# The start of the second attention lane in a two-layer decoder kernel, tied to the first lane by an event, with a shorter stated latency for one norm

## The chip, the cores and the metric

The kernel runs on one core of a Trainium2 chip. The metric is the time of one execution on the device in microseconds (us). The engines of the core run side by side, each through its own queue of instructions, and wait for one another by semaphores: PE (TensorE, matrix products and transposes), DVE (VectorE), ACT (ScalarE), POOL (GpSimd) and SP (SyncE, which here only starts transfers).

## The reference

A stack of two layers over 256 positions of width 1024. Each layer adds to the residual stream, every time behind an RMS norm: half a gated feed-forward, a mixer, a cross attention over 256 memory tokens, and half a second feed-forward. The mixer is the part that the change touches:

```
z = h @ w_in                     # one projection: HGRN2 q|f|i|g, FoX q|k|v, forget logits
o_h = hgrn2_chunk_scan(...)      # 4 heads, then a norm per head and a gate
s = q k^T / 8 + (c_t - c_s)      # FoX: 8 heads x 64, c = running sum of log forget gates
o_f = softmax(causal(s)) v
x += concat(o_h, o_f) @ w_out
# cross attention, on the same x:
x += softmax(rms_norm(x) wq (rms_norm(mem) wk)^T / 16) (rms_norm(mem) wv) wo
```

## The kernel before

Everything is computed in float32 on PE with the operands split in two parts, a high and a low one, so that each product is three matmuls (`mm3`, L455 to L457; L455 uses both high parts, L456 and L457 a low one). The weights are loaded in pieces of 1 MB by SP (tiles `raw`, 3 buffers, L145). ACT casts a piece to the high part (`whi`, L158, or L162 when a gain is multiplied in) and DVE takes the difference as the low part (`wlo`, L159 or L163); 7 buffers of each. Activations are split alike by `put_split` (L380): the high part by ACT (L381), the low part by DVE (L382). So `xfh`/`xfl`, `oTh`/`oTl`, `mfh`/`mfl` (the memory's features) and the two halves of `kc` (the cross attention's keys) come about.

The causal FoX attention works on pairs of heads. Two tasks, the lanes, run `fox_lane`: lane 0 takes pair 0 and then pair 2, lane 1 pairs 1 and 3. For a pair a lane stacks its operands (`fox_stack`), makes the scores of two heads (`fs`, L966, one small PSUM tile for each head), takes the row maxima on DVE (`fmx`, L973, which is also the last reader of `fs`) and negates them (`fnm`, L977), takes exponentials on ACT (L928), reciprocals (`frc`, L930) and the normalisation of the probabilities `pp` on DVE (L932), transposes them on PE (`fpt`, L984), copies the transposes by ACT (`ppT`, L987), multiplies by the values (`fpv`, L997 to L999) and splits the result into `oTh`/`oTl`. The HGRN2 heads end beside it (L868 on DVE, transposes `hot`, L874).

While the lanes work, the mixer's main task fills PE with products for the cross attention, which need only the memory: keys (`acc` of 128x256, then `kc`) and values (`acc` of 128x512). Then come the product with `w_out`, the residual, and the norm for the cross attention, one `norm_task` for each half of the positions: square, gain and inverse root, then after a stated latency the transposes (`to_feat`, `pt`, L375) and the split into `xfh`/`xfl`.

The order of the instructions on every engine is that of recording. `drive` lets tasks take turns by a virtual clock that only counts PE's time: a task that yields a number moves the clock on, one that yields a tuple sleeps for that many microseconds while others record (a stated latency), and one that yields an `Event` sleeps until it is fired, and `fire(lat)` wakes it `lat` after the clock at that moment. So a constant such as `LAT_LANE` or `LAT_X` costs no time itself; it sets what is recorded ahead of what. Within this order a scheduler puts some norm and split instructions earlier on their engines (`tc.high_priority`). The small PSUM tiles (`fs`, `fpt`, `fpv`, `hot`, `pt` and others) share 4 buffers in turn, so each waits until the fourth before it has been read for the last time.

Before the change lane 1 sleeps after its first `fox_stack` for `LAT_FK + LAT_LANE` = 6.5 + 2.8, lane 0 for 6.5, each from when it was recorded itself.

## Time and profile before

| | us |
|---|---|
| median of 3 runs | 1210.65 |
| lowest and highest of them | 1210.35, 1213.19 |
| the profiled execution | 1210.42 |
| its span, first to last instruction | 1208.6 |
| PE busy | 1194.0 |
| DVE busy | 769.2 |
| ACT busy | 651.4 |
| POOL busy | 37.7 |

The mean granted clock of TensorE was 0.999 of full speed. A row of the timeline gives start, duration, engine, source line, operation, the tile written and those read, the shape and how many instructions were merged; a bracket tells how long the engine sat idle ahead of it and who released it. Matmuls are pipelined: one of 128x256 lasts 0.28 us but the next starts 0.11 us after it, so stalls on PE are read from the starts. Layer 0's mixer attention lies at about 295 to 330 us, its norm at 343 to 367; layer 1's at about 885 to 926 and 938 to 962.

### The profile page before, as it was taken

The numbers are of one execution on the slowest core, as the hardware profiler recorded it, in microseconds if no ns is written. First come the engines' busy times: TensorE is split into PE (matmuls) and PEld (weight loads), VectorE is DVE, ScalarE is ACT, GpSimd is POOL, SyncE is SP. The second block draws the span as 40 slices with busy tenths as digits, with TensorE's granted clock in tenths as the row PEclk, the third lists the DMA queues.
The fourth block names the chain that finished last, engine by engine and source line by source line (L and its number), as shares of the span: only waits on it lengthen the run. The fifth ranks groups of instructions, "written<-read, shape, count | busy, mean of one in ns | idle before, by whom it ended". The sixth has DMA issues, their size and how long they took to land.

```text
span 1208.6 us, 21485 instructions
## 1 busy us (share of the span) xinstructions
PE 1194.0 (99%) x8989; PEld 1094.6 (91%) x8989; DVE 769.2 (64%) x1194; ACT 651.4 (54%) x1022; POOL 37.7 (3%) x50
## 2 busy tenths in 40 slices
PE   9999999999999999999999999999999999999997
PEld 7999888989889889998889998889988898999986
DVE  6866647488866675565474565476787766555643
ACT  7556535578854464454354454266687555444532
POOL 0000000011000000000000000000110000000000
PEclk9999999999999999999999999999999999999999
DMA  8655655544444374565474666464445533555750
GB/s 300 226 192 177 240 175 185 184 142 140 166 165 175 105 261 145 204 214 205 139 259 143 209 209 210 139 222 163 145 154 169 190 130 137 192 194 175 244 174 36
DMA packets 100001, 218.66 MB, mean 181 GB/s; under 512 B 4128, under 2 KB 16704, under 8 KB 99904
## 3 DMA queue, kind: packets, MB, share of 16 engines
q1 hardware_dynamic: 99744, 217.03, 53.0%
q8 instruction: 70, 1.15, 0.4%
q10 hardware_dynamic: 160, 0.27, 0.1%
q14 instruction: 27, 0.22, 0.1%
HBM read 216.23 MB, written 1.05 MB: 180 GB/s over the span
## 4 chain that ended last, share of the span: by engine, by line
PE 86%; DVE 6%; ACT 4%; issue 2%; DMA 2%; POOL 1%; POOLq 0%; SPq 0%; ACTq 0%; DVEq 0%
PE acc L455 26%; PE acc L456 26%; PE acc L457 26%; DVE wlo L159 2%; ACT whi L162 1%; DVE wlo L163 1%; PE acc L520 1%; DMA mem<-in_mem_dram 1%; PE pt L375 1%; DMA raw<-in_w_in_dram 1%; POOL rs L356 1%; ACT whi L158 1%; DVE xfl L382 0%; PE al L797 0%; ACT pp L928 0%
## 5 line engine op out<-in xcount | busy, mean ns | idle before, releaser
L159 DVE TENSOR_TENSOR wlo<-raw,whi 128x1024 fp32r<-128x1024 f32 (+1 forms) x332 | 389.8, 1196 | 256.6 <-ACT whi L158 247.8
L158 ACT CAST whi<-raw 128x1024 fp32r<-128x1024 f32 (+1 forms) x332 | 331.8, 1030 | 258.8 <-PE acc L457 148.6
L457 PE MATMUL acc<-xfh,wlo 128*128 128x256 f32 x1536 | 424.4, 276 | 1.4 <-DVE wlo L159 1.3
L455 PE MATMUL acc<-xfh,whi 128*128 128x256 f32 x1536 | 425.6, 277 | 0.0
L456 PE MATMUL acc<-xfl,whi 128*128 128x256 f32 x1536 | 424.3, 276 | 0.7 <-DVE xfl L382 0.7
L457 PEld LDWEIGHTS acc<-xfh,wlo 128*128 128x128 f32 x1536 | 288.3, 188 | 2.0 <-DVE wlo L159 2.0
L456 PEld LDWEIGHTS acc<-xfl,whi 128*128 128x128 f32 x1536 | 288.4, 188 | 1.4 <-DVE xfl L382 1.1
L455 PEld LDWEIGHTS acc<-xfh,whi 128*128 128x128 f32 x1536 | 288.4, 188 | 0.9 <-ACT whi L158 0.2
L455 PE MATMUL acc<-whi,hth 128*128 128x512 f32 (+1 forms) x352 | 136.9, 389 | 0.0
L457 PE MATMUL acc<-whi,htl 128*128 128x512 f32 (+1 forms) x352 | 136.4, 387 | 0.0
L456 PE MATMUL acc<-wlo,hth 128*128 128x512 f32 (+1 forms) x352 | 136.3, 387 | 0.0
L455 PE MATMUL acc<-whi,xfh 128*128 128x512 f32 (+1 forms) x240 | 87.5, 365 | 0.0
L457 PE MATMUL acc<-whi,xfl 128*128 128x512 f32 (+1 forms) x240 | 86.8, 362 | 0.0
L456 PE MATMUL acc<-wlo,xfh 128*128 128x512 f32 (+1 forms) x240 | 86.6, 361 | 0.0
L457 PEld LDWEIGHTS acc<-whi,htl 128*128 128x128 f32 x352 | 66.1, 188 | 13.6
L456 PEld LDWEIGHTS acc<-wlo,hth 128*128 128x128 f32 x352 | 66.1, 188 | 13.2
L455 PEld LDWEIGHTS acc<-whi,hth 128*128 128x128 f32 x352 | 66.1, 188 | 13.2
L163 DVE SCALAR_TENSOR_TENSOR wlo<-raw,g,whi 128x512 fp32r<-128x512 f32 (+1 forms) x96 | 62.0, 701 | 20.9 <-ACT whi L162 20.9
L162 ACT ACTIVATE whi<-raw,g 128x512 fp32r<-128x512 f32 (+1 forms) x96 | 58.3, 677 | 19.3 <-PE acc L456 15.2
L457 PEld LDWEIGHTS acc<-whi,xfl 128*128 128x128 f32 x240 | 45.1, 188 | 7.3
L381 ACT CAST hth<-sil 128x512 fp32r<-128x512 f32 x36 | 22.3, 620 | 54.0 <-DVE sil L760 53.9
L456 PEld LDWEIGHTS acc<-wlo,xfh 128*128 128x128 f32 x240 | 45.2, 188 | 6.8
(274 smaller groups left out, 1520.3 us busy)
## 6 DMA issues: line engine op xcount, KB each, us to landing
raw<-in_ffn_w_down_dram SPq DMA_DIRECT2D x44, 1024.0 KB, 5.0
raw<-in_ffn_w_up_dram SPq DMA_DIRECT2D x40, 1024.0 KB, 5.4
raw<-in_ffn_w_gate_dram SPq DMA_DIRECT2D x38, 1024.0 KB, 5.2
raw<-in_w_in_dram SPq DMA_DIRECT2D x24, 1024.0 KB, 5.3
raw<-in_cross_wk_dram SPq DMA_DIRECT2D x8, 1024.0 KB, 5.2
raw<-in_cross_wv_dram SPq DMA_DIRECT2D x8, 1024.0 KB, 5.3
raw<-in_w_out_dram SPq DMA_DIRECT2D x8, 1024.0 KB, 4.9
raw<-in_cross_wq_dram SPq DMA_DIRECT2D x8, 1024.0 KB, 5.1
```

The lines of the kernel that those rows point to most:

```text
L158: nc.scalar.copy(out=hi, in_=sl)
L159: nc.vector.tensor_tensor(out=lo, in0=sl, in1=hi.bitcast(F32), op=ALU.subtract)
L162: nc.scalar.mul(hi, sl, g)
L163: nc.vector.scalar_tensor_tensor(out=lo, in0=sl, scalar=g, in1=hi.bitcast(F32), op0=ALU.mult, op1=ALU.subtract)
L356: nc.gpsimd.tensor_tensor(out=rs, in0=ms, in1=neghalf[:, 0:1], op=ALU.pow)
L375: nc.tensor.transpose(pt[:, j * P:(j + 1) * P], hn[:, kt * P:(kt + 1) * P], ident)
L381: nc.scalar.copy(out=hi, in_=src)
L455: nc.tensor.matmul(ps, lhsT=lh, rhs=rh, start=start, stop=False)
L456: nc.tensor.matmul(ps, lhsT=lh, rhs=rl, start=False, stop=False)
L457: nc.tensor.matmul(ps, lhsT=ll, rhs=rh, start=False, stop=stop)
L520: nc.tensor.matmul(psa_[t], lhsT=x, rhs=w, start=kt == 0 and which == 0, stop=kt == KT - 1 and which == 1)
```

## The change

Two things change. The norm behind the mixer is created with a stated latency of 5.3 in place of 6.5. And lane 1, before its first scores, sleeps 6.5 like lane 0 and then waits for an event that lane 0 fires when its own first scores and softmax are recorded, with a latency of 2.0; the stated 2.8 is gone.

```
-LAT_NORM, LAT_X = 5.5, 6.5
+LAT_NORM, LAT_X = 5.5, 5.3
...
-LAT_FK, LAT_LANE = 6.5, 2.8
+LAT_FK, LAT_LANE = 6.5, 2.0
...
-    def fox_lane(lane, fq, fk, fv, L_, R_, oT, cmask, oh, ready, done):
+    def fox_lane(lane, fq, fk, fv, L_, R_, oT, cmask, oh, ready, done, ahead):
         yield ready
         for pr in (lane, lane + 2):
             qs, ks = fox_stack(pr, fq, fk, L_, R_, oh)
-            yield (LAT_FK + LAT_LANE * (pr == 1),)
+            yield (LAT_FK,)
+            if pr == 1:
+                yield ahead
             prs = []
             for sub in range(2):
                 ps = smp("fs")
...
                 softmax(pr_, nmx, 1.0, [(t, pr_[:, o:o + n], pr_[:, o:o + n]) for t, o, n in SEGS])
+            if pr == 0:
+                ahead.fire(LAT_LANE)
             yield (LAT_FS,)
...
+        ahead = Event()
         for lane in range(2):
-            spawn(fox_lane(lane, fq, fk, fv, L_, R_, oT, cmask, oh, ev_g, ev_p))
+            spawn(fox_lane(lane, fq, fk, fv, L_, R_, oT, cmask, oh, ev_g, ev_p, ahead))
```

No instruction is added or removed on any engine; their order moves on PE, DVE, ACT and SP. Lines of the changed kernel below the lanes' first change are 2 to 5 higher: L966 becomes L968, L973 L975, L977 L979, L984 L988.

The first place is DVE in layer 0, second pair: the rows between the maxima of lane 1 (heads' probabilities `pp_526` and `pp_532`) and their normalisations L932. Before:

```order
L163 SCALAR_TENSOR_TENSOR wlo_543_3855<-raw_491_3580,gmem_202_1659,whi_542_3854 128x512
L977 TENSOR_SCALAR fnm_534_3818<-fmx_533_3815 128x2
L163 SCALAR_TENSOR_TENSOR wlo_543_3855<-raw_491_3580,gmem_202_1659,whi_542_3854 128x512
L159 TENSOR_TENSOR wlo_554_3911<-raw_496_3594,whi_553_3910 128x1024
L930 RECIPROCAL frc_530_3805<-fsm_529_3802 128x2
L930 RECIPROCAL frc_536_3823<-fsm_535_3820 128x2
L932 TENSOR_SCALAR pp_526_3796<-pp_526_3796,frc_530_3805 128x128
L932 TENSOR_SCALAR pp_526_3796<-pp_526_3796,frc_530_3805 128x256
L932 TENSOR_SCALAR pp_532_3814<-pp_532_3814,frc_536_3823 128x128
L932 TENSOR_SCALAR pp_532_3814<-pp_532_3814,frc_536_3823 128x256
L382 TENSOR_TENSOR kc_433_3270<-acc_512_3721,kc_432_3269 128x512
L159 TENSOR_TENSOR wlo_556_3915<-raw_496_3594,whi_555_3914 128x1024
```

After:

```order
L163 SCALAR_TENSOR_TENSOR wlo_543_3855<-raw_491_3580,gmem_202_1659,whi_542_3854 128x512
L979 TENSOR_SCALAR fnm_534_3821<-fmx_533_3818 128x2
L159 TENSOR_TENSOR wlo_554_3911<-raw_496_3594,whi_553_3910 128x1024
L930 RECIPROCAL frc_530_3808<-fsm_529_3805 128x2
L159 TENSOR_TENSOR wlo_556_3915<-raw_496_3594,whi_555_3914 128x1024
L932 TENSOR_SCALAR pp_526_3799<-pp_526_3799,frc_530_3808 128x128
L932 TENSOR_SCALAR pp_526_3799<-pp_526_3799,frc_530_3808 128x256
L930 RECIPROCAL frc_536_3826<-fsm_535_3823 128x2
L382 TENSOR_TENSOR kc_433_3270<-acc_512_3721,kc_432_3269 128x512
L932 TENSOR_SCALAR pp_532_3817<-pp_532_3817,frc_536_3826 128x128
L932 TENSOR_SCALAR pp_532_3817<-pp_532_3817,frc_536_3826 128x256
```

A second weight split (`wlo_556`) and the split of `kc_433` now stand ahead of the last two L932, and the reciprocal of the second head stands behind the first head's L932.

The second place is layer 1, first pair, on PE: the scores of lane 0 (`fs_1365`, `fs_1371`) and of lane 1. Before:

```order
L966 MATMUL fs_1365_9605<-fks_1340_9449,fqs_1339_9448 128x128 x2
L966 MATMUL fs_1365_9605<-fks_1340_9449,fqs_1339_9448 128x256 x2
L966 MATMUL fs_1371_9623<-fks_1340_9449,fqs_1339_9448 128x128 x2
L966 MATMUL fs_1371_9623<-fks_1340_9449,fqs_1339_9448 128x256 x2
L966 MATMUL fs_1377_9641<-fks_1342_9465,fqs_1341_9464 128x128 x2
L966 MATMUL fs_1377_9641<-fks_1342_9465,fqs_1341_9464 128x256 x2
L966 MATMUL fs_1383_9659<-fks_1342_9465,fqs_1341_9464 128x128 x2
L966 MATMUL fs_1383_9659<-fks_1342_9465,fqs_1341_9464 128x256 x2
L455 MATMUL acc_1389_9679<-mfh_1265_8775,whi_1328_9392 128x256
L456 MATMUL acc_1389_9679<-mfl_1266_8776,whi_1328_9392 128x256
L457 MATMUL acc_1389_9679<-mfh_1265_8775,wlo_1329_9393 128x256
```

After, from 18 matmuls behind lane 0's scores on (lane 1's are `fs_1378` and `fs_1384` now):

```order
L455 MATMUL acc_1377_9643<-mfh_1267_8777,whi_1346_9488 128x256
L456 MATMUL acc_1377_9643<-mfl_1268_8778,whi_1346_9488 128x256
L457 MATMUL acc_1377_9643<-mfh_1267_8777,wlo_1347_9489 128x256
L968 MATMUL fs_1378_9665<-fks_1342_9465,fqs_1341_9464 128x128 x2
L968 MATMUL fs_1378_9665<-fks_1342_9465,fqs_1341_9464 128x256 x2
L968 MATMUL fs_1384_9683<-fks_1342_9465,fqs_1341_9464 128x128 x2
L968 MATMUL fs_1384_9683<-fks_1342_9465,fqs_1341_9464 128x256 x2
L455 MATMUL acc_1377_9643<-mfh_1267_8777,whi_1346_9488 128x256
L456 MATMUL acc_1377_9643<-mfl_1268_8778,whi_1346_9488 128x256
L457 MATMUL acc_1377_9643<-mfh_1267_8777,wlo_1347_9489 128x256
```

Lane 1's scores stood right behind lane 0's; now 21 matmuls of the keys' product lie between. In the same place on DVE, from lane 1's first normalisation (`pp_1378` before, `pp_1379` after) to the first split of the next weight; `wlo_1396` is the low part of the last weight block of the keys' product that PE works on there. Before:

```order
L932 TENSOR_SCALAR pp_1378_9646<-pp_1378_9646,frc_1382_9655 128x128
L932 TENSOR_SCALAR pp_1378_9646<-pp_1378_9646,frc_1382_9655 128x256
L163 SCALAR_TENSOR_TENSOR wlo_1396_9753<-raw_1343_9480,gmem_202_1659,whi_1395_9752 128x512 x2
L930 RECIPROCAL frc_1388_9673<-fsm_1387_9670 128x2
L932 TENSOR_SCALAR pp_1384_9664<-pp_1384_9664,frc_1388_9673 128x128
L932 TENSOR_SCALAR pp_1384_9664<-pp_1384_9664,frc_1388_9673 128x256
L382 TENSOR_TENSOR oTl_1357_9565<-hot_1390_9713,oTh_1356_9564 128x4x128
L382 TENSOR_TENSOR oTl_1357_9565<-hot_1391_9720,oTh_1356_9564 128x4x128
L382 TENSOR_TENSOR kc_1336_9445<-acc_1389_9679,kc_1335_9444 128x512
L163 SCALAR_TENSOR_TENSOR wlo_1399_9761<-raw_1348_9494,gmem_202_1659,whi_1398_9760 128x512 x2
```

After:

```order
L163 SCALAR_TENSOR_TENSOR wlo_1396_9753<-raw_1343_9480,gmem_202_1659,whi_1395_9752 128x512
L930 RECIPROCAL frc_1383_9679<-fsm_1382_9676 128x2
L932 TENSOR_SCALAR pp_1379_9670<-pp_1379_9670,frc_1383_9679 128x128
L932 TENSOR_SCALAR pp_1379_9670<-pp_1379_9670,frc_1383_9679 128x256
L930 RECIPROCAL frc_1389_9697<-fsm_1388_9694 128x2
L932 TENSOR_SCALAR pp_1385_9688<-pp_1385_9688,frc_1389_9697 128x128
L932 TENSOR_SCALAR pp_1385_9688<-pp_1385_9688,frc_1389_9697 128x256
L382 TENSOR_TENSOR oTl_1357_9565<-hot_1390_9713,oTh_1356_9564 128x4x128
L382 TENSOR_TENSOR oTl_1357_9565<-hot_1391_9720,oTh_1356_9564 128x4x128
L382 TENSOR_TENSOR kc_1336_9445<-acc_1377_9643,kc_1335_9444 128x512
L163 SCALAR_TENSOR_TENSOR wlo_1396_9753<-raw_1343_9480,gmem_202_1659,whi_1395_9752 128x512
```

The second half of `wlo_1396` stood ahead of the last two normalisations and now stands behind them, both `oTl` and the split of `kc`.

The third place is PE at the norm behind the mixer, layer 0, second half of the positions (the transposes `pt_614` and `pt_615`; layer 1 and the first half alike). Before:

```order
L457 MATMUL acc_599_4149<-whi_601_4152,mfl_349_2551 128x512
L455 MATMUL acc_598_4148<-whi_603_4158,mfh_348_2550 128x512
L456 MATMUL acc_598_4148<-wlo_604_4159,mfh_348_2550 128x512
L457 MATMUL acc_598_4148<-whi_603_4158,mfl_349_2551 128x512
L455 MATMUL acc_599_4149<-whi_603_4158,mfh_348_2550 128x512
L456 MATMUL acc_599_4149<-wlo_604_4159,mfh_348_2550 128x512
L457 MATMUL acc_599_4149<-whi_603_4158,mfl_349_2551 128x512
L375 MATMUL pt_614_4228<-ident_101,hn_605_4170 128x128 x4
L375 MATMUL pt_615_4235<-ident_101,hn_605_4170 128x128 x4
L455 MATMUL acc_598_4148<-whi_603_4158,mfh_348_2550 128x512
L456 MATMUL acc_598_4148<-wlo_604_4159,mfh_348_2550 128x512
```

After:

```order
L457 MATMUL acc_599_4149<-whi_601_4152,mfl_349_2551 128x512
L375 MATMUL pt_614_4222<-ident_101,hn_605_4170 128x128 x4
L375 MATMUL pt_615_4229<-ident_101,hn_605_4170 128x128 x4
L455 MATMUL acc_598_4148<-whi_603_4158,mfh_348_2550 128x512
L456 MATMUL acc_598_4148<-wlo_604_4159,mfh_348_2550 128x512
L457 MATMUL acc_598_4148<-whi_603_4158,mfl_349_2551 128x512
L455 MATMUL acc_599_4149<-whi_603_4158,mfh_348_2550 128x512
L456 MATMUL acc_599_4149<-wlo_604_4159,mfh_348_2550 128x512
L457 MATMUL acc_599_4149<-whi_603_4158,mfl_349_2551 128x512
L455 MATMUL acc_598_4148<-whi_603_4158,mfh_348_2550 128x512
L456 MATMUL acc_598_4148<-wlo_604_4159,mfh_348_2550 128x512
```

The transposes stand six matmuls of 128x512 earlier. On ACT and DVE the splits into `xfh` and `xfl` now stand ahead of the casts and splits of the third piece of `cross_wq` (`whi_626`, `wlo_627`), and on SP the load of the next gain vector (`wn`) ahead of the load of that piece.

Further moves of the same kind: in layer 0 the first scores, transposes and value products of lane 1 and its second scores stand three matmuls of 128x256 later; in its first pair the split `kc_431` and one negation stand on DVE ahead of lane 1's second maximum. In layer 1 lane 1's first transposes stand 24 matmuls behind lane 0's (before 3), its value products 18 behind (before adjacent), its second scores behind six matmuls of 128x512 more, its second transposes 12 of these behind lane 0's and the value products 6 behind (both adjacent before).

## Rows read from the trace of the kernel before

**Rows 1.** The page of the profile: its first line, PE's busy time with its share of the span and its count of instructions, and the shares of engines in the chain of work that ended last.

```profile
span 1208.6 us, 21485 instructions
...
PE 1194.0 (99%) x8989; PEld 1094.6 (91%) x8989; DVE 769.2 (64%) x1194; ACT 651.4 (54%) x1022; POOL 37.7 (3%) x50
...
PE 86%; DVE 6%; ACT 4%; issue 2%; DMA 2%; POOL 1%; POOLq 0%; SPq 0%; ACTq 0%; DVEq 0%
```

**Rows 2.** The list of waits of PE: for what it waited, in all (us), how often, and the longest.

```profile
PE fs L966 <- DVE AX L868: 1.0, 1, 1.0
PE acc L456 <- DVE xfl L382: 0.7, 2, 0.4
PE fpt L984 <- DVE oTl L382: 0.7, 1, 0.7
...
PE fpv L997 <- ACT ppT L987: 0.3, 1, 0.3
```

**Rows 3.** The timeline of PE at the norm behind the mixer, layer 0.

```profile
364.70 1.04 PE L375 MATMUL pt<-ident,hn 128*128 128x128 f32 x8
...
366.96 0.40 PE L455 MATMUL acc<-xfh,whi 128*128 128x256 f32 x2
367.72 0.39 PE L456 MATMUL acc<-xfl,whi 128*128 128x256 f32 x1 [0.36 <-DVE xfl L382]
```

**Rows 4.** The timeline of DVE at the same place.

```profile
361.30 5.76 DVE L159 TENSOR_TENSOR wlo<-raw,whi 128x1024 fp32r<-128x1024 f32 x5
366.98 1.28 DVE L382 TENSOR_TENSOR xfl<-pt,xfh 128x512 fp32r<-128x512 f32 x2
```

**Rows 5.** The timeline of SP at the same place: the issue of the load of the next gain vector.

```profile
358.87 0.34 SPq L350 DMA_DIRECT2D wn<-in_ffn_norm_dram  x1
```

**Rows 6.** The timeline of PE in layer 0: the lanes' first pairs, and below the second.

```profile
298.88 0.84 PE L984 MATMUL fpt<-ident,pp 128*128 128x128 f32 x6
299.47 0.36 PE L455 MATMUL acc<-mfh,whi 128*128 128x256 f32 x1
...
303.50 0.43 PE L997 MATMUL fpv<-ppT,fv 128*64 128x128 f32 x2
...
304.57 0.38 PE L455 MATMUL acc<-mfh,whi 128*128 128x256 f32 x1
...
306.29 0.28 PE L457 MATMUL acc<-mfh,wlo 128*128 128x256 f32 x1
306.87 0.43 PE L997 MATMUL fpv<-ppT,fv 128*64 128x128 f32 x2 [0.30 <-ACT ppT L987]
...
323.98 0.82 PE L984 MATMUL fpt<-ident,pp 128*128 128x128 f32 x6
324.55 0.47 PE L455 MATMUL acc<-whi,mfh 128*128 128x512 f32 x1
```

**Rows 7.** The timeline of DVE in layer 0: the first pairs, and below the second.

```profile
298.69 0.42 DVE L973 CUSTOM_DVE_ANT_0 pp<-fs,cmask 128x256 f32<-128x256 f32 x1
...
299.32 0.67 DVE L382 TENSOR_TENSOR kc<-acc,kc 128x512 fp32r<-128x512 f32 x1
...
321.94 1.22 DVE L159 TENSOR_TENSOR wlo<-raw,whi 128x1024 fp32r<-128x1024 f32 x1
...
323.26 1.01 DVE L932 TENSOR_SCALAR pp<-pp,frc 128x128 f32<-128x128 f32 x4
324.19 0.68 DVE L382 TENSOR_TENSOR kc<-acc,kc 128x512 fp32r<-128x512 f32 x1
324.79 4.62 DVE L159 TENSOR_TENSOR wlo<-raw,whi 128x1024 fp32r<-128x1024 f32 x4
```

**Rows 8.** The timeline of PE in layer 1: the first pairs, and the transposes of the second.

```profile
886.18 1.17 PE L966 MATMUL fs<-fks,fqs 128*128 128x128 f32 x8
888.40 1.28 PE L966 MATMUL fs<-fks,fqs 128*128 128x128 f32 x8 [1.05 <-DVE AX L868]
...
897.18 0.28 PE L457 MATMUL acc<-mfh,wlo 128*128 128x256 f32 x1
898.17 1.14 PE L984 MATMUL fpt<-ident,pp 128*128 128x128 f32 x6 [0.72 <-DVE oTl L382]
899.08 0.36 PE L455 MATMUL acc<-mfh,whi 128*128 128x256 f32 x1
...
902.00 0.43 PE L997 MATMUL fpv<-ppT,fv 128*64 128x128 f32 x2
...
903.73 0.39 PE L455 MATMUL acc<-mfh,whi 128*128 128x256 f32 x1
...
918.66 1.47 PE L984 MATMUL fpt<-ident,pp 128*128 128x128 f32 x12
```

**Rows 9.** The timeline of DVE in layer 1: the first pairs, and below the second.

```profile
895.45 1.41 DVE L163 SCALAR_TENSOR_TENSOR wlo<-raw,gmem,whi 128x512 fp32r<-128x512 f32 x2
...
898.63 0.68 DVE L382 TENSOR_TENSOR kc<-acc,kc 128x512 fp32r<-128x512 f32 x1
899.24 2.73 DVE L163 SCALAR_TENSOR_TENSOR wlo<-raw,gmem,whi 128x512 fp32r<-128x512 f32 x4
...
918.79 0.54 DVE L932 TENSOR_SCALAR pp<-pp,frc 128x128 f32<-128x128 f32 x2
919.25 3.49 DVE L159 TENSOR_TENSOR wlo<-raw,whi 128x1024 fp32r<-128x1024 f32 x3
```

## The prediction

> **What bounds the kernel now.** I read the page first: TensorE (PE) is busy 99% of the 1208.6 us span and holds 86% of the chain of waits [rows 1]. No matmul is added or removed, so the time can change only by the few microseconds in which PE waits, and by new waits of the same kind. The list of PE's waits comes second [rows 2]: it holds some 8 us, and four of its entries lie where the change moves something: the scores (fs) behind L868, the transposed probabilities (fpt) behind L382, the values product (fpv) behind ppT, and the first matmuls of the cross attention behind xfl, twice. Third I read the timelines around these places, PE's and VectorE's (DVE's) side by side. There I count a stall from start to start: what lies between two starts beyond the usual distance (0.113 us for a 128x256 matmul, 0.227 us for a 128x512 one), since the idle time printed in brackets begins only when the modelled end of the matmul ahead has passed.
>
> **Part 1, the norm behind the mixer (both layers).** In layer 0 the first cross matmuls start at 366.96 as a pair, and the L456 that needs xfl at 367.72 [rows 3]. Without a wait it would have come some 0.12 us after the pair's second, so about 0.64 us are lost: the end of the chain transposes, xfh on ScalarE (ACT), xfl on DVE. The change puts the transposes six 128x512 matmuls earlier, 6 x 0.227 = 1.36 us, from 364.70 to about 363.34. Then xfh is ready by about 365.0. xfl doesn't gain all of that, for DVE works through five weight splits from 361.30 to 366.98, 1.13 each [rows 4], and four of them stay ahead of xfl: 361.30 + 4 x 1.13 = 365.8; the first half of xfl ends at some 366.4, ahead of the 367.1 at which PE asks. The fifth split (wlo_627) now stands behind xfl and comes 1.2 us later; it belongs to the second block of columns, 96 matmuls x 0.114 = 10.9 us behind the first, which covers it. On SP's queue the next gain vector (wn) goes ahead of the third load of cross_wq; wn can't be sent before the norm has read the old vector (it went at 358.87) [rows 5], so that load goes out some 3 us later. Its cast is now behind xfh on ACT, so nothing of the norm is queued behind it, and the same 10.9 us hide it; without that cover it would cost up to 3 us. The gain: 0.64 in each layer, **-1.28 us**. Bounds: -1.28 (the whole wait), and 0 if xfl stays behind all five splits.
>
> **Part 2, layer 0, the lanes.** The first and second scores of lane 1 move only three 128x256 matmuls (0.34 us) back, but the queue of DVE changes more than PE's. *First pair.* The PSUM slot that lane 0's second transposes (fpt) take is lane 1's second scores'; it comes free with lane 1's second maximum (L973). Before, that began at 298.69 and freed the slot by about 299.05; PE was at this fpt, the second half of a group that runs from 298.88 to 299.47, at 299.17 [rows 6, 7]: just met. Now a split of kc (0.60, as from 324.19 to 324.79) and a negation (under 0.1) stand ahead of it on DVE, and the scores come 0.34 later: 299.05 + 0.60 + 0.07 + 0.34 = 300.05, a new wait of 0.88. The old wait of lane 1's fpv (306.29 to 306.87, less 0.11: 0.47) [rows 6] shrinks, since PE gets there later while ppT is held by ACT's casts, by my working to 0.23. Net 0.88 - 0.24 = **+0.64**. *Second pair.* Before, lane 1's normalisations (L932) ran on DVE from 323.26 to 324.2, just in time for PE's fpt at 323.98 [rows 6, 7]: there is no slack. Now the split wlo_556 (1.13) and the kc split (0.60) stand between the maxima and the last of those L932, and the whole chain starts 0.64 + 0.14 = 0.78 later, as PE does: 324.27 + 1.13 + 0.60 + 0.78 = 326.78, and the matmul behind fpt, which was at 324.55, starts at about 327.0. Layer 0 in all, with the first pair's 0.64 in it: **+2.45 us**. Bounds: if DVE uses the time in which it waits for the exponentials for the split, 1.13 goes from the sum and +1.3 is left; the upper bound is 2.7, with 0.25 more for exponentials that wait for the cast of that weight on ACT. I take the upper half, because the old rows show the L932 just met, and DVE with no gap printed ahead of a row from the split at 321.94 to the one at 324.79.
>
> **Part 3, layer 1, the lanes.** *First pair, what goes.* Before, the scores of both lanes stand back to back; lane 1's need the slot that L868 frees, and start at 888.40 where 887.18 was possible: 1.22. The fpt at 898.17 wait for oTl: 0.88 there and 0.27 within them, for the matmul behind them comes at 899.08 instead of 0.64 after the start [rows 8]. After the change lane 1's scores stand 21 matmuls (2.4 us) later, at about 889.6, when the slot has been free for 1.2 us; and its fpt stand 21 later too, behind the end of oTl. So 2.37 us go. *What comes.* DVE's queue holds the second half of the split wlo_1396 behind all four softmaxes, both oTl and kc, where it stood ahead of them before. The same work ended at 899.24 before [rows 9]; with lane 1's scores later I put it at 899.8. PE, counted on from the scores at 889.6 (1.0 for them, 12 + 18 + 24 matmuls by 0.115, 0.8 for the eight L874, 0.6 for six fpt), asks for it at 898.2: a new wait of 1.6. Two groups of 12 fpv in place of one of 24 cost 2 x 1.07 - 1.73 = 0.41 (1.07 from 303.50 to 304.57, 1.73 from 902.00 to 903.73) [rows 6, 8]. By this chain lane 0's fpv start at 901.48 instead of 902.00: -0.52 + 0.41 = **-0.1**; bounds -0.7 (wlo_1396 at 899.2) and +0.3 (at 900.2). *Second pair.* Before, one group of 12 fpt waits for nothing [rows 8]; lane 1's last L932 ran at 918.79 [rows 9]. Now lane 1's scores are behind six 128x512 matmuls more and its fpt 12 (2.7 us) behind lane 0's, with three splits of 1.13 among the normalisations. I put the last L932 at 923.3, and PE there at 922.4: +0.8. The fpv are separated again: +0.45. Layer 1 in all **+1.2 us**; bounds 0 (every wait just met: -0.7 + 0.45, and half the 0.8 hidden) and +2.
>
> **Sum.** +2.45 + 1.2 - 1.28 = +2.4 us. The profiled execution took 1210.42 us, 0.23 below the median of the three runs (1210.65), so I forecast 1210.42 + 2.4 = **1212.8 us**. Smallest sum of these bounds 1.3 + 0 - 1.28 = 0.0, largest 2.7 + 2.0 - 0 = 4.7.
>
> **Rivals.** *A, the forecast:* about +0.5 to +3.6, at 1212.8. *B, the waits go and nothing takes their place.* For it: four waits of 0.3 to 1.2 us are removed by plain moves. Against it: PE's next need lies close behind DVE's delivery at each place [rows 7, 9]. Time: -0.47 - 2.37 - 1.28 + 0.41 + 0.45 = -3.3, 1207.1 us; without the norm's gain 1208.4. The gap at 888.40 is a wait for a PSUM slot, as the row's releaser L868 (the last reader of that slot) says [rows 8]. The Trainium skill (Perfetto Trace Analysis, § Optimization Strategy) says of gaps on the engine that should be saturated to find what they wait for and to make that start sooner, and that the same gap repeating can mean that there isn't enough SBUF or PSUM for the next tile. By that rule, ordering the slot's new user behind its release gains the gap whole, and the time would be B's; here the gap is there once in two layers, so the trace bears out the slot, not the repetition. *C, it comes out even:* the new waits give back what goes, within 1 us: 1210.4. *D, slower.* DVE's queue is served in order, and the change lets weight splits and kc stand ahead of normalisations in the second pair of both layers. If that costs in layer 1 what I reckon for layer 0 (1.13 + 0.60 + 0.6 for a later start, and 0.45 for the fpv, 2.8 instead of 1.25) and the first pair there +0.3 instead of -0.1, the sum is 2.7 + 3.1 - 1.28 = +4.5, 1214.9 us. It decides from the point where lane 1's last normalisation in layer 1 is more than about 2 us behind PE. For it: the last normalisation there is followed at once by three more splits, 919.25 on [rows 9], so DVE is as full as in layer 0. Against it: PE has 12 more matmuls (2.7 us) ahead of lane 1's fpt there, which layer 0 doesn't get. *E, the change does nothing to be seen,* as the norm's stated latency would do if xfl stayed behind all splits: only part 1 goes, and the sum is +3.7, 1214.1 us; it is the upper end of A.
>
> **How the numbers follow.** A 0.55 (of it 0.03 above +3.6), B 0.20, C 0.13, D 0.12. About 0.3%, 3.6 us, is what a measurement of this kernel can tell from no change. Faster than that needs nearly all of B: 0.04. Slower: D and the end of A, 0.15. Within: 0.81. The range leaves out the faster half of B (0.10) and the far side of D and E (0.07): 1208.0 to 1215.0. The likeliest case's own range is 1210.9 to 1214.0.
>
> **What would show it.** Right: in layer 0 PE waits for a normalisation (L932) ahead of the second pair's fpt by some 2 us, and for a maximum ahead of the first pair's; in layer 1 no wait at fs or fpt of the first pair, but one of about 1.6 at an L457 behind the split by L163, and one under 1 us at the last fpt; L456 behind xfl is gone from the list in both layers. Wrong: if the L932 of layer 0's second pair is not a releaser of PE, part 2 is void and B or C holds; if L932 waits 2 us and more in layer 1 too, D; if xfl is still in the list, part 1. A wait for a DMA of cross_wq would show that the load moved on SP's queue isn't hidden.

## The result and the profile after

The changed kernel takes 1211.83 us (median of 20 runs, 1210.66 to 1214.47), the kernel before 1210.14 (20 runs, 1208.83 to 1213.19). The ratio is 1.0015, with a 95% interval of 1.0009 to 1.0021: 1.1 to 2.5 us slower, so the change is a small loss, within the 0.3% that the forecast took for what a measurement can tell. The profiled execution took 1211.08 us. PE's row of its page, against [rows 1]:

```profile
PE 1194.8 (99%) x8989; PEld 1094.5 (91%) x8989; DVE 770.5 (64%) x1194; ACT 651.1 (54%) x1022; POOL 36.8 (3%) x50
```

PE is as busy as before, and its list of waits shows other names than [rows 2]:

```profile
PE acc L457 <- DVE wlo L163: 1.2, 2, 0.7
PE fpt L988 <- DVE pp L932: 1.1, 2, 0.7
PE acc L455 <- ACT whi L162: 0.9, 1, 0.9
PE fpt L988 <- DVE fmx L975: 0.7, 1, 0.7
```

The entries of before for fs behind L868, fpt behind oTl, L456 behind xfl and fpv behind ppT are gone. These four stand there instead; of the first, 0.5 was there before, and the 0.7 is new. The timeline of PE in layer 0, first pair, second pair and norm, against [rows 3, 6]:

```profile
297.55 0.49 PE L988 MATMUL fpt<-ident,pp 128*128 128x128 f32 x3
298.77 0.55 PE L988 MATMUL fpt<-ident,pp 128*128 128x128 f32 x3 [0.73 <-DVE fmx L975]
...
323.13 0.39 PE L457 MATMUL acc<-whi,mfl 128*128 128x512 f32 x1
324.20 0.70 PE L988 MATMUL fpt<-ident,pp 128*128 128x128 f32 x3 [0.69 <-DVE pp L932]
325.32 0.70 PE L988 MATMUL fpt<-ident,pp 128*128 128x128 f32 x3 [0.41 <-DVE pp L932]
325.77 0.47 PE L455 MATMUL acc<-whi,mfh 128*128 128x512 f32 x1
...
328.71 0.43 PE L1001 MATMUL fpv<-ppT,fv 128*64 128x128 f32 x2
...
330.44 0.50 PE L455 MATMUL acc<-whi,mfh 128*128 128x512 f32 x1
...
367.80 0.28 PE L455 MATMUL acc<-xfh,whi 128*128 128x256 f32 x1
367.91 0.28 PE L456 MATMUL acc<-xfl,whi 128*128 128x256 f32 x1
```

And DVE at the same three places, against [rows 4, 7]:

```profile
297.62 0.69 DVE L382 TENSOR_TENSOR kc<-acc,kc 128x512 fp32r<-128x512 f32 x1
...
298.29 0.42 DVE L975 CUSTOM_DVE_ANT_0 pp<-fs,cmask 128x256 f32<-128x256 f32 x1
...
322.74 1.21 DVE L159 TENSOR_TENSOR wlo<-raw,whi 128x1024 fp32r<-128x1024 f32 x1
323.86 0.55 DVE L932 TENSOR_SCALAR pp<-pp,frc 128x128 f32<-128x128 f32 x2
...
324.39 0.68 DVE L382 TENSOR_TENSOR kc<-acc,kc 128x512 fp32r<-128x512 f32 x1
324.98 0.55 DVE L932 TENSOR_SCALAR pp<-pp,frc 128x128 f32<-128x128 f32 x2
...
361.24 4.62 DVE L159 TENSOR_TENSOR wlo<-raw,whi 128x1024 fp32r<-128x1024 f32 x4
365.78 1.28 DVE L382 TENSOR_TENSOR xfl<-pt,xfh 128x512 fp32r<-128x512 f32 x2
```

*First pair.* Three transposes take 0.3 us, but the fourth starts 1.22 after the first: 0.92 lost, because the split of kc (297.62) stands ahead of the maximum at 298.29 that frees the slot. *Second pair.* The transposes should have started at 323.36, and six should have taken 0.57. They start at 324.20 and are over at 325.77: 0.84 + 1.00 = 1.84 lost. DVE shows why: a split, L932, the split of kc, and the second L932 at 324.98. *Norm.* xfl now starts at 365.78, behind four splits, and L456 follows the L455 ahead of it by 0.11: no wait.

PE in layer 1, first pair and the last transposes of the second, against [rows 8]:

```profile
886.44 1.17 PE L968 MATMUL fs<-fks,fqs 128*128 128x128 f32 x8
...
889.84 1.09 PE L968 MATMUL fs<-fks,fqs 128*128 128x128 f32 x8
...
897.73 0.28 PE L457 MATMUL acc<-mfh,wlo 128*128 128x256 f32 x1
898.91 0.39 PE L455 MATMUL acc<-mfh,whi 128*128 128x256 f32 x1 [0.91 <-ACT whi L162]
899.13 0.28 PE L456 MATMUL acc<-mfl,whi 128*128 128x256 f32 x1
900.10 0.38 PE L457 MATMUL acc<-mfh,wlo 128*128 128x256 f32 x1 [0.68 <-DVE wlo L163]
900.32 0.29 PE L455 MATMUL acc<-mfh,whi 128*128 128x256 f32 x1
...
901.78 0.43 PE L1001 MATMUL fpv<-ppT,fv 128*64 128x128 f32 x2
...
902.90 0.39 PE L455 MATMUL acc<-mfh,whi 128*128 128x256 f32 x1
...
905.17 0.43 PE L1001 MATMUL fpv<-ppT,fv 128*64 128x128 f32 x2
...
906.24 0.38 PE L455 MATMUL acc<-mfh,whi 128*128 128x256 f32 x1
...
922.72 0.82 PE L988 MATMUL fpt<-ident,pp 128*128 128x128 f32 x6
```

DVE, against [rows 9], and then ACT at the first of these places:

```profile
897.50 1.28 DVE L382 TENSOR_TENSOR oTl<-hot,oTh 128x512 fp32r<-128x512 f32 x2
898.70 0.68 DVE L382 TENSOR_TENSOR kc<-acc,kc 128x512 fp32r<-128x512 f32 x1
899.30 3.40 DVE L163 SCALAR_TENSOR_TENSOR wlo<-raw,gmem,whi 128x512 fp32r<-128x512 f32 x5
...
922.26 0.55 DVE L932 TENSOR_SCALAR pp<-pp,frc 128x128 f32<-128x128 f32 x2
```

```profile
896.71 1.05 ACT L381 CAST oTh<-hot 128x512 fp32r<-128x512 f32 x2
897.65 0.58 ACT L381 CAST kc<-acc 128x512 fp32r<-128x512 f32 x1
898.13 3.19 ACT L162 ACTIVATE whi<-raw,gmem 128x512 fp32r<-128x512 f32 x5
```

Both waits of [rows 8] are gone: lane 1's scores start at 889.84 and find their slot free. Instead L455 waits for the high part of the weight (898.91, where 897.85 was possible) and L457 for the low part (900.10, where 899.25 was possible): 1.06 + 0.85 = 1.91 us, against the 2.37 that went. On DVE the low part stands behind oTl and kc, and on ACT the high part stands behind oTh and kc in the same way. Of the two it is DVE's queue that sets the time: L455 has the high part at 898.91, while DVE turns to the low part only at 899.30, so L457 would have waited until 900.10 also without the wait of L455. In the second pair the last L932 (922.26, with 0.55 for its two instructions) is over at 922.81. It belongs to the last three of the six transposes, which begin at about 923.0 (half of the 0.57 from 922.72 to the next product at 923.29): no wait, with some 0.2 us to spare.

**What each stage costs.** Single executions differ by some us at places that no edit touches: the trace of before has a wait of 0.6 at an L797 behind kk, which one of the other traces has too, with 0.3, and the rest don't have, and between 200 and 287 us that trace falls 0.7 to 1.7 us behind every other one, whatever was changed. So spans are not compared here. I took each matmul that both traces hold, and how much later it starts than in the trace of before; the median over 3 us of such matmuls ahead of a stage is subtracted from the one behind it. That is the stage's cost in us. The stages: L0 is 290 to 340 us of the trace of before (in brackets its first part, to 311, with the first pair), N0 340 to 376, L1 880 to 933 (first part to 907), N1 940 to 972. All runs in one table, with the times beside them:

| kernel | L0 (first pair) | N0 | L1 (first pair) | N1 | median, before beside it | ratio, 95% interval |
|---|---|---|---|---|---|---|
| after | +2.17 (+0.72) | -0.63 | +1.01 (+0.25) | -0.63 | 1211.83, 1210.14 | 1.0015, 1.0009 to 1.0021 |
| e1_norm | +0.07 | -0.63 | -0.06 | -0.63 | 1208.42, 1209.82 | 0.9987, 0.9979 to 0.9996 |
| e2_event | +2.14 (+0.69) | +0.01 | +0.99 (+0.23) | 0.00 | 1213.07, 1209.82 | 1.0030, 1.0018 to 1.0042 |
| e3_event_l0 | +2.15 (+0.72) | +0.01 | -0.06 | +0.01 | 1211.62, 1209.82 | 1.0017, 1.0008 to 1.0026 |
| e4_event_l1 | +0.08 | +0.01 | +0.86 (+0.21) | 0.00 | 1211.84, 1209.82 | 1.0014, 1.0006 to 1.0023 |
| f0_max_first | +0.89 (+0.69) | -0.63 | +0.99 (+0.23) | -0.63 | 1209.84, 1210.37 | 0.9999, 0.9990 to 1.0008 |
| h1_later_fpt | +1.44 (+0.72) | -0.63 | +0.97 (+0.23) | -0.63 | 1210.86, 1210.37 | 1.0005, 0.9997 to 1.0014 |
| m1_l1_12 | +0.14 | -0.61 | +1.07 (+0.03) | -0.63 | 1209.53, 1210.37 | 0.9992, 0.9983 to 1.0001 |
| m2_l1_6 | -0.11 | -0.63 | +0.03 (-0.01) | -0.63 | 1208.66, 1210.37 | 0.9987, 0.9979 to 0.9996 |
| k1_kc_later | +1.66 (-0.02) | -0.63 | +0.50 (-0.25) | -0.63 | 1210.09, 1209.43 | 1.0007, 0.9998 to 1.0016 |
| d1_kc_twice | +2.13 (+0.83) | -0.63 | +1.05 (+0.30) | -0.63 | 1211.73, 1209.43 | 1.0016, 1.0007 to 1.0025 |
| h3_norm_4 | +0.08 | -0.63 | +0.01 | -0.63 | 1207.99, 1209.43 | 0.9992, 0.9983 to 1.0001 |

For the change the stages give 2.17 - 0.63 + 1.01 - 0.63 = +1.9 us, and the medians 1211.83 - 1210.14 = +1.7. The ratio is worked out from runs side by side, so it isn't exactly the quotient of the two medians. Two cautions for the table. Each row's stages come from one trace; where an edit leaves a stage of the lanes alone they come out between -0.11 and +0.14, so differences of that size are not read. And for f0_max_first, h1_later_fpt, m1_l1_12, k1_kc_later and h3_norm_4 the interval of the ratio takes in 1: what is said of the parts of the stages there rests on the traces, which the times don't contradict but are too coarse to confirm.

### The profile page after: what moved, and what is told of

Its sections match the earlier page's. It is cut to its first block, busy times and chain, and to the rows that moved or that the text cites. A ratio compares the mean times of both kernels' runs of the same rounds, so it can differ in the third digit from the quotient of the medians.

```text
span 1209.3 us, 21482 instructions
## 1 busy us (share of the span) xinstructions
PE 1194.8 (99%) x8989; PEld 1094.5 (91%) x8989; DVE 770.5 (64%) x1194; ACT 651.1 (54%) x1022; POOL 36.8 (3%) x50
## 3 DMA queue, kind: packets, MB, share of 16 engines
HBM read 216.23 MB, written 1.05 MB: 180 GB/s over the span
## 4 chain that ended last, share of the span: by engine, by line
PE 87%; ACT 5%; DVE 4%; issue 2%; DMA 1%; POOL 1%; POOLq 0%; SPq 0%; ACTq 0%; DVEq 0%
PE acc L455 27%; PE acc L457 27%; PE acc L456 27%; ACT whi L162 1%; PE acc L520 1%; PE pt L375 1%; DVE wlo L159 1%; DMA mem<-in_mem_dram 1%; DVE wlo L163 1%; ACT pp L928 1%; ACT whi L158 1%; PE al L797 0%; ACT fqs L945 0%; PE cpo L456 0%; POOL hrs L866 0%
## 5 line engine op out<-in xcount | busy, mean ns | idle before, releaser
L455 PE MATMUL acc<-xfh,whi 128*128 128x256 f32 x1536 | 425.8, 277 | 0.0
L457 PE MATMUL acc<-xfh,wlo 128*128 128x256 f32 x1536 | 424.3, 276 | 1.3 <-DVE wlo L159 1.3
L456 PE MATMUL acc<-xfl,whi 128*128 128x256 f32 x1536 | 424.1, 276 | 0.0
L457 PEld LDWEIGHTS acc<-xfh,wlo 128*128 128x128 f32 x1536 | 288.4, 188 | 1.7 <-DVE wlo L159 1.7
L455 PEld LDWEIGHTS acc<-xfh,whi 128*128 128x128 f32 x1536 | 288.4, 188 | 0.7
L456 PEld LDWEIGHTS acc<-xfl,whi 128*128 128x128 f32 x1536 | 288.4, 188 | 0.4
L455 PE MATMUL acc<-whi,hth 128*128 128x512 f32 (+1 forms) x352 | 137.0, 389 | 0.0
L457 PE MATMUL acc<-whi,htl 128*128 128x512 f32 (+1 forms) x352 | 136.4, 387 | 0.0
L456 PE MATMUL acc<-wlo,hth 128*128 128x512 f32 (+1 forms) x352 | 136.3, 387 | 0.0
L455 PE MATMUL acc<-whi,xfh 128*128 128x512 f32 (+1 forms) x240 | 87.5, 365 | 0.0
L457 PE MATMUL acc<-whi,xfl 128*128 128x512 f32 (+1 forms) x240 | 86.9, 362 | 0.0
L456 PE MATMUL acc<-wlo,xfh 128*128 128x512 f32 (+1 forms) x240 | 86.6, 361 | 0.0
L457 PEld LDWEIGHTS acc<-whi,htl 128*128 128x128 f32 x352 | 66.1, 188 | 13.5
L456 PEld LDWEIGHTS acc<-wlo,hth 128*128 128x128 f32 x352 | 66.1, 188 | 13.3
L455 PEld LDWEIGHTS acc<-whi,hth 128*128 128x128 f32 x352 | 66.1, 188 | 13.3
L457 PEld LDWEIGHTS acc<-whi,xfl 128*128 128x128 f32 x240 | 45.1, 188 | 7.2
L456 PEld LDWEIGHTS acc<-wlo,xfh 128*128 128x128 f32 x240 | 45.2, 188 | 6.9
L455 PEld LDWEIGHTS acc<-whi,xfh 128*128 128x128 f32 x240 | 45.1, 188 | 6.9
```

The costliest lines, as they stand in the source:

```text
L455: nc.tensor.matmul(ps, lhsT=lh, rhs=rh, start=start, stop=False)
L456: nc.tensor.matmul(ps, lhsT=lh, rhs=rl, start=False, stop=False)
L457: nc.tensor.matmul(ps, lhsT=ll, rhs=rh, start=False, stop=stop)
```

## Experiments: the parts of the change

The theory is the forecast's: the event costs in both layers, since DVE's order puts splits ahead of what PE asks for, and the norm gives some of it back. The rival is B, that the waits go and nothing comes. First the norm alone (in before) and the event alone (in after):

```
e1_norm:   -LAT_NORM, LAT_X = 5.5, 6.5
           +LAT_NORM, LAT_X = 5.5, 5.3
e2_event:  -LAT_NORM, LAT_X = 5.5, 5.3
           +LAT_NORM, LAT_X = 5.5, 6.5
```

e1_norm:

> Only the norm's stated latency changed, 6.5 to 5.3; the lanes as before. Theory (the change is a sum of parts that don't touch each other): the wait for xfl goes in both layers, 2 x 0.64, so -1.3 us against the kernel before (ratio 0.9989), and xfl is gone from PE's list of waits. Rival (the norm's gain is eaten by the load of cross_wq that goes out later on SP): 0, and a wait on the DMA or on the third piece's cast appears. Second rival (the parts interact, and the norm only gains behind the shifted lanes): between -0.3 and 0.

e2_event:

> Only the lanes' event; the norm's latency stays 6.5. Theory (sum of parts, read from the trace of the changed kernel): layer 0 +2.2, layer 1 +1.05, the xfl waits stay: +3.2 us (ratio 1.0027). Rival (interaction): the whole change's +1.8, or less, since the norm would then not have paid anything back.

The norm alone gives 0.63 in each layer, 1.26 us, and 1208.42 against 1209.82 in time. Its list of PE's waits has no xfl, and the lanes' waits of [rows 2] are still there, fs behind L868 with 1.0 and fpt behind oTl with 0.8.

The event alone costs 2.14 + 0.99 = 3.1 us by the stages and 3.25 by the medians. So the change is a loss and a gain that don't touch one another, as far as the stages can tell, and the gain alone is the faster kernel.

Then the event in one layer only, with the norm as before:

```
e3_event_l0: +        ahead = Event() if l == 0 else None
e4_event_l1: +        ahead = Event() if l == 1 else None
both:        +            yield (LAT_FK + 2.8 * (pr == 1 and ahead is None),)
             +            if pr == 1 and ahead is not None:
             +                yield ahead
```

e3_event_l0:

> The event in layer 0 alone, layer 1's lanes as before, the norm's latency 6.5. Theory: +2.2 us, 0.7 of it at the first pair (fpt behind a maximum) and 1.5 at the second (fpt behind normalisations). Rival (the loss is made in layer 1, where the scores move farthest): 0.

e4_event_l1:

> The event in layer 1 alone, layer 0's lanes as before, the norm's latency 6.5. Theory: +1.05 us: 2.37 of old waits gone, 1.92 of new ones at the weight split, the rest for groups of transposes and value products that stand apart now. Rival (in layer 1 old and new waits even out, and the groups apart cost nothing): -0.4 to 0. Rival of the forecast on record: +1.2 with a wait of 0.8 at the last fpt.

Each layer's cost stands in its own stage alone: +2.15 in layer 0, +0.86 in layer 1, together 3.0 of the 3.1 of e2_event. By the medians it is 1.8 and 2.0; the interval for layer 1, 0.7 to 2.8 us, holds both readings. Both layers lose: B is out for layer 1 too, though its two waits did go.

## Experiments: what PE waits for in layer 0

f0_max_first gives the maxima of lane 1 in the first pair of layer 0 a higher priority (HP is the offset that the kernel uses elsewhere), so that on DVE they stand ahead of kc:

```
+                with tc.high_priority(offset=HP * (ahead.first and pr == 1)):
                     for t, o, n in SEGS:
                         nc.vector.tensor_tensor_reduce(...)
...
+        ahead.first = l == 0
```

> The changed kernel, with the maxima of lane 1's first pair in layer 0 given priority. PE's order is that of the changed kernel; on DVE those maxima now stand ahead of the kc split, and, as the scheduler's order follows from it, the weight split wlo_556 of the second pair stands behind the last normalisation again, and its cast on ACT behind lane 1's exponentials; the kc split stays ahead of the last two normalisations. Theory (layer 0's loss is made by DVE's order): the first pair's wait of 0.95 falls to 0.3 or less, the second pair's 1.9 to about 0.6 (the kc split), so layer 0 costs +0.6 in place of +2.2 and the whole is at +0.2 against the kernel before (ratio 1.0002). Rival (it is PE's order: scores, transposes and products of lane 1 standing apart): nothing changes, +1.8, with the same waits behind other releasers.

DVE, first and second pair, and PE there:

```profile
297.20 0.67 DVE L382 TENSOR_TENSOR kc<-acc,kc 128x512 fp32r<-128x512 f32 x1
297.79 0.54 DVE L932 TENSOR_SCALAR pp<-pp,frc 128x128 f32<-128x128 f32 x2
...
322.80 0.67 DVE L382 TENSOR_TENSOR kc<-acc,kc 128x512 fp32r<-128x512 f32 x1
323.39 0.54 DVE L932 TENSOR_SCALAR pp<-pp,frc 128x128 f32<-128x128 f32 x2
323.84 2.35 DVE L159 TENSOR_TENSOR wlo<-raw,whi 128x1024 fp32r<-128x1024 f32 x2
```

```profile
298.12 0.70 PE L989 MATMUL fpt<-ident,pp 128*128 128x128 f32 x3 [0.40 <-DVE pp L932]
...
323.15 1.27 PE L989 MATMUL fpt<-ident,pp 128*128 128x128 f32 x6
324.17 0.47 PE L455 MATMUL acc<-whi,mfh 128*128 128x512 f32 x1
```

The first pair stayed at +0.69, which wasn't expected. kc no longer stands ahead of the maximum, but it and the maxima now stand ahead of lane 0's normalisation (L932 at 297.79), and the same transposes wait for that, 0.40 in the bracket. The second pair changed with it, for the order of the weights' work moved too: the second split (wlo_556) runs at 323.84, behind the last L932, and the transposes take 1.02 in place of 0.57. Of 1.84 lost, 0.45 is left, and the second pair's cost falls from 1.45 to 0.20. So the split ahead of L932 is most of what the second pair pays for, as the forecast said.

h1_later_fpt leaves DVE as it is and lets PE ask later: lane 1's transposes of the second pair stand six matmuls of 128x512 further back.

```
-            yield (LAT_FS,)
+            yield (LAT_FS + 1.3 * (pr == 3),)
```

> The changed kernel, with lane 1's transposes of the second pair six 128x512 matmuls (1.36 us) later; DVE's and ACT's order in layer 0 is that of the changed kernel. Theory (in layer 0 PE waits there for a normalisation that DVE brings late): 1.36 of the 1.9 us go, in layer 1, where PE doesn't wait at that place, nothing; +0.45 against the kernel before (ratio 1.0004). Rival (the normalisation's lateness is followed by one of the products fpv, so the wait only moves on): +1.8, with a wait of fpv behind ppT.

The six transposes and what is lost at them now take 1.05 in place of 0.57, so 0.5 is lost where it was 1.84: some 1.36 less, what six matmuls take (6 x 0.227). But the stage gains 0.73 only. The value products, 24 in one group of 1.73 in after (328.71 to 330.44), now stand in two groups of 12, of 1.08 and 1.07 us, and the second costs 0.1 more ahead of it and 0.1 behind it: 0.6 is given back.

k1_kc_later puts the split of kc 40 places back in both layers:

```
+                with tc.high_priority(offset=-40):
+                    put_split(kc[c][0][:, sl, :], kc[c][1][:, sl, :], ...)
```

> The changed kernel, with the split of the keys (kc) put back by 40 places of priority, so that on DVE it stands behind lane 1's second maximum in layer 0's first pair, and behind the second half of wlo_1396 in layer 1; PE's order is that of the changed kernel. Theory (kc is what makes these two deliveries late): layer 0's first wait of 0.95 falls to 0.2 or 0.3, the waits at the weight split in layer 1 fall from 1.9 to 1.3; about +0.4 against the kernel before (ratio 1.0003). Rival (other work takes kc's place, for DVE has enough of it): +1.8, with the same waits.

In layer 0 the first pair's cost goes from +0.72 to -0.02, and the lost time at the transposes from 0.92 to 0.35; in layer 1 the stage falls by half. There PE waits less at both weights:

```profile
PE acc L457 <- DVE wlo L163: 1.1, 2, 0.6
PE acc L455 <- ACT whi L162: 0.5, 1, 0.5
```

So kc ahead of the maximum is the first pair's cost in layer 0, and in layer 1 kc ahead of the weight is a part of it. The second pair of layer 0, where DVE's order is that of after, isn't relieved, as it should be if wlo_556 causes its cost: it has +1.68 in place of +1.45, since PE, no longer held up in the first pair, waits the longer there. By the stages the whole is therefore at +0.9 and not at the +0.4 that was expected.

## Experiments: layer 1

m1_l1_12 and m2_l1_6 keep the event in layer 1 alone, with the shorter norm, and let lane 1's scores follow by 12 and by 6 matmuls of 128x256 where the change has 21:

```
m1_l1_12: -LAT_FK, LAT_LANE = 6.5, 2.0
          +LAT_FK, LAT_LANE = 6.5, 1.0
m2_l1_6:  +LAT_FK, LAT_LANE = 6.5, 0.5
both:     +        ahead = Event() if l == 1 else None   (and the lines under "both" above)
```

> The norm at 5.3; the event in layer 1 alone, fired with 1.0, so that lane 1's first scores stand 12 matmuls (1.36 us) behind lane 0's there instead of none before or 21 in the change. Theory: the wait for the slot (1.22) goes; DVE's order still has the second half of wlo_1396 behind oTl and kc, so most of the 1.9 at the weight split comes; two groups of fpv more, 0.35: layer 1's lanes at +0.6 to +1.0, the whole, with the norm's -1.3, at -0.5 (ratio 0.9996). Rival (the loss of layer 1 comes from the scores standing too far behind): layer 1's lanes at -0.8, the whole at -2.1 (0.9983).

> The same with 0.5: lane 1's first scores 6 matmuls (0.68 us) behind lane 0's in layer 1. Theory: 0.68 of the 1.22 go at the scores, the weight split is as late as in the run before, since DVE has the same order: layer 1's lanes at +0.8 to +1.3, the whole at -0.2 (ratio 0.9998). Rival: layer 1's lanes at -0.5, the whole at -1.8 (0.9985).

With 12 matmuls the waits of the first pair are 0.89 at fpt behind oTl, 0.72 at fpv behind ppT and 0.29 at L457: 1.9 in all, each counted from start to start. With 6 they are 0.52 at the scores, 0.83 at fpt and 0.44 at fpv: 1.8. I had expected a cost of 0.8 to 1.3 us for the second, and it has none; there the low part of the weight is not what PE waits for. Its list has fs behind L868, fpt behind oTl and fpv behind ppT.

The second pair of m1_l1_12 has the wait that I had forecast for the change: 1.02 at fpt behind L932, and the stage costs +1.07. In m2_l1_6, where the value products of the second pair also stay in one group, that wait is not there.

d1_kc_twice changes after: in layer 1 the low part of each block of the first kc is computed twice on DVE, with the same values, to see what 0.6 us more of work there do. One of the two additions (896.08 in its trace) lies in the stretch ahead of PE's waits, the other (904.00) behind it.

```
+                if l == 1 and c == 0:
+                    nc.vector.tensor_tensor(out=kc[c][1][:, sl, :], in0=ps.rearrange(...),
+                                            in1=kc[c][0][:, sl, :].bitcast(F32), op=ALU.subtract)
```

> The changed kernel, with the split of the keys' first two blocks in layer 1 done twice on DVE (the same values written again, 2 x 0.60 us of work); in DVE's new order both halves of wlo_1396 stand ahead of lane 1's normalisations again, as before the change. Theory A (in layer 1 PE waits for the whole of DVE's work in that stretch, whichever piece comes last): no wait at the weight split any more but one as long at the transposes, behind oTl or a normalisation, and 0.6 longer: layer 1's lanes at +1.6 in place of +1.05, +2.4 in all against the kernel before (ratio 1.0020). Theory B (the place of wlo_1396 is the cause): the waits at the split go and 0.6 to 1.0 of other ones come, layer 1's lanes at 0 to +0.3, +0.9 in all (ratio 1.0007).

Neither expectation was met: the stage costs +1.05, as in after. The extra instruction moved the order. Both halves of wlo_1396 now stand ahead of lane 1's normalisations, and PE's waits at the weight are gone. In their place fpt and fpv wait, which were free in after:

```profile
PE fpv L1001 <- ACT ppT L991: 1.2, 1, 1.2
```

```profile
902.00 2.57 ACT L162 ACTIVATE whi<-raw,gmem 128x512 fp32r<-128x512 f32 x4
904.46 1.61 ACT L991 COPY ppT<-fpt 128x384 f32<-128x384 f32 x4
```

From start to start they are 0.29 + 0.18 + 0.27 at the transposes and 1.38 at the value products: 2.1 us. The larger one is not DVE's: on ACT four casts of the next weight (902.00) stand ahead of the copies ppT. So the run gives no price for one more kc split; it shows that with the weight's split first on DVE, PE waits at other places. The first pair's waits in layer 1 add up to 2.37 in before, 1.91 in after, 1.9, 1.8 and 2.1 in these three, with five different sets of names. Only k1_kc_later, which takes work out of that stretch, has less: 1.4 at the weight and 0.16 elsewhere. What sets the sum stays open: the amount of work on DVE alone doesn't, for d1_kc_twice has 0.6 us more of it in the stretch, and its sum is 0.2 above that of after.

Last, e1_norm with a still shorter norm, LAT_X = 4.0:

> The norm at 4.0 in place of 5.3, the lanes as before: its transposes stand six 128x512 matmuls earlier still. Theory (the wait for xfl is gone already at 5.3): the same as at 5.3, -1.3 us (ratio 0.9989). Rival (the earlier transposes meet the norm's end, so that PE waits for hn): -0.5 to -1.0, with pt behind hn in the list of waits.

The two norms give 0.63 each, as with 5.3: the wait was all that there was to gain. No version here is faster than e1_norm by more than the measurement can tell; m2_l1_6, with the event in layer 1, has the same ratio as e1_norm without it.

## Why the prediction was right

The time was forecast as +2.4 us and is +1.7, as rival A had it; C, within 1 us, lies just outside the interval of 1.1 to 2.5. By its steps:

- **Norm, right, with luck in two numbers.** -1.28 forecast, -1.26 measured in both stages. xfl passed the fifth split, so E, in which it doesn't, is out. The later load and cast of cross_wq cost nothing: no wait for them is in the list. The 365.78 at which xfl starts equals the 365.8 that was reckoned by chance: PE runs 0.84 later there in the trace of after (367.80 against 366.96), so on the clock of before xfl came 0.9 earlier than reckoned. And the 0.64 counts the usual 0.12 as lost; by the forecast's own words (0.12 behind the pair's second, which starts at 367.08) the wait is 0.52. The rest is made up by the matmul behind it, which came 0.22 later (367.72 to 367.94) in place of 0.12.
- **Layer 0, first pair, right.** +0.64 forecast, +0.72 measured. The wait behind the second maximum was put at 0.88 and is 0.92, and k1_kc_later shows that kc is its cause.
- **Layer 0, second pair, the wait right and the sum too high.** The wait was reckoned with 1.13 + 0.60 for the two splits and measures 1.84; f0_max_first shows the larger term. The sum was +1.81 and is +1.45, for one term was missing: the kernel before lost 0.40 inside its value products there (below), which don't wait any more. The old list of waits doesn't name them.
- **Layer 1, first pair, mis-sized.** -0.1 forecast, +0.25 measured. Up to the value products the chain was right: lane 0's were put at 901.48, and they run at 901.78 in a trace that is 0.26 later there (lane 0's scores at 886.44 against 886.18), so at 901.52. What was too small is the price of two groups, 0.41: they take 1.12 + 1.07 where one takes 1.73, and the second costs 0.1 more ahead of it and 0.1 behind it, nearly 0.7 in all. 901.52 - 902.00 + 0.7 = +0.2. The wait itself was mis-sized too, 1.6 where 1.91 came, without an effect on the sum: the forecast counted 24 matmuls between lane 0's transposes and that L457, the rows have 20, so PE asked some 0.4 earlier for a low part that came when it was reckoned (899.8 on the clock of before). (That is also why the forecast's -2.37 + 1.6 + 0.41 gives -0.36 and not its -0.1, which goes by the chain.) The high part I had not followed through ACT's queue, where it stands behind the exponentials, oTh and kc; that gave one of the two waits its name, but cost nothing more.
- **Layer 1, second pair, mis-sized the other way.** The wait of 0.8 at the last transposes isn't there. The last L932 was put at 923.3; it was over at 922.81 in a trace that is 0.7 later there, more than 1 us earlier than reckoned. The forecast doesn't show the terms of its 923.3, so which of them was too long stays open. The stage's second part costs 0.76, of which the separated value products are some 0.5 (0.45 forecast); the other 0.2 stands in no single row. D, with 2 us and more at L932, didn't come, though the margin at the last transposes was only some 0.2: m1_l1_12 has a wait of 1.02 there.
- **Rival B fell** although every wait it named did go. The releaser in the rows was right: L868 freed the slot of lane 1's scores, and with the scores later the wait is gone in after and m1_l1_12 and shorter in m2_l1_6. The Trainium skill (Perfetto Trace Analysis, § Optimization Strategy) tells the reader to look for what blocks a gap and to make that start sooner or end faster. The trace agrees with the wording, for the norm is such a case: its transposes were put earlier, and its gap went whole. The event makes nothing start sooner; it moves the one that waits, and in layer 1 1.91 of 2.37 us came back under other names.

So the two layers lose in different ways. In layer 0 DVE's new order makes waits that weren't there. In layer 1 the waits even shrink a little (1.91 for 2.37), and the rows put the loss at the value products, which the change parts in both pairs (0.7 + 0.5). m2_l1_6 fits: with the event in layer 1, but the second pair's products in one group, that layer costs +0.03. No run put the first pair's together again with the event in place, so for that pair this is a sum of rows and not shown by an experiment.

The sums err by +0.36 in layer 0's second pair, by -0.35 in layer 1's first pair and by +0.49 in its second, so the forecast owes some of its accuracy to errors that cancel.

The rows of before for the 0.40, PE in layer 0 and then ACT:

```profile
327.47 0.43 PE L997 MATMUL fpv<-ppT,fv 128*64 128x128 f32 x2
...
328.41 0.43 PE L997 MATMUL fpv<-ppT,fv 128*64 128x128 f32 x2
...
329.60 0.50 PE L455 MATMUL acc<-whi,mfh 128*128 128x512 f32 x1
```

```profile
326.94 1.05 ACT L158 CAST whi<-raw 128x1024 fp32r<-128x1024 f32 x1 [0.28 <-DMA raw<-in_w_out_dram]
327.89 0.85 ACT L987 COPY ppT<-fpt 128x384 f32<-128x384 f32 x2
```

24 value products begin at 327.47 and the next product starts at 329.60, 2.13 us, where the group of after takes 1.73; nothing between has a bracket. The 13th, the first of lane 1, starts at 328.41. The first of its copies ppT is over at about 328.36, for on ACT the cast of a weight stands ahead of it. So this is a wait for ppT, hidden from the list because the modelled ends of the matmuls overlap it. The other traces bear it out: with layer 0's lanes as before the group takes 1.90 to 2.28 us (e1_norm, e4_event_l1, m1_l1_12, m2_l1_6, h3_norm_4), and 1.73 with the event in layer 0 (after, e2_event, e3_event_l0, f0_max_first, k1_kc_later, d1_kc_twice).

## What to carry to other kernels

Where PE waited for another engine's queue, moving the one that waits mostly changed the name of the wait (layer 1); what shortened it was work that started earlier (the norm) or left that stretch of the queue (kc). And what is parted by the move has a price of its own. Before a wait is taken away, write out what stands in order on every engine that feeds the place (here DVE and ACT both) and see what is just met next. A change with two parts is worth measuring in parts: here one gave 1.3 us and the other took 3.

## What the runs showed that was not expected

- Splitting a group of 24 small value products in two cost 0.5 to 0.7 us: 1.08 + 1.07 against 1.73 (h1_later_fpt), 1.12 + 1.07 against 1.73 (after, layer 1), and in both some 0.2 more around the second group.
- The matmul behind one that waited came about 0.22 us after it in place of 0.11 (898.91 to 899.13 and 900.10 to 900.32 in after), so each wait cost about 0.1 more than its own length.
- A priority for the maxima of one pair (f0_max_first) also changed which split stands ahead of which normalisation 25 us further on, and that was the larger effect: 0.03 us in the pair, 1.25 behind it.
- The waits of one stretch added up to 1.8 to 2.4 us in four orders of the same work, and to 2.1 in a fifth with 0.6 us more of it on DVE.
